# Where the operands of the split products lie in SBUF: staggered slots of 520 columns, weight buffers of 1032

## The chip, the cores and the metric

The kernel runs on one core of one Trainium2 chip. The metric is the device time of one execution in microseconds (us).

## The reference

Two layers of a decoder trunk over 512 tokens of 1024 features, and a last RMSNorm, all in float32. In each layer:

```
n = RMSNorm(h)
p = n @ W_in                                  # 1024 -> 4256 columns
y_A = RWKV7_time_mix(p_A) @ W_oA              # 8 heads x 64, delta-rule state
y_B = MLA(p_B) @ W_oB                         # 8 heads, low-rank q / kv, causal softmax
h = h + (sigmoid(g_A) * y_A + sigmoid(g_B) * y_B) @ W_out
u_gate, u_val = split(RMSNorm(h) @ W_ffn_up)  # 1024 -> 2 x 2816
h = h + (gelu(causal_conv3(u_gate) + b) * u_val) @ W_ffn_down   # 2816 -> 1024
```

## The kernel before, in words

Features lie on the 128 partitions and tokens along the free dimension, so a matrix of activations is a row of tiles of 128x512. Every large product (W_in, the up- and output projections, W_out, the two products of the FFN) is a **split product**: both operands are cut into a high part that TensorE's float32r form holds exactly and a low part, the rest, and one product of a 128x128 weight block with a 128x512 tile of activations becomes three matmuls, `hi·whi`, `lo·whi`, `hi·wlo`, which `mm3` issues in this order (lines 246, 247, 248). In each of them the weight block is the operand loaded into the array (LDWEIGHTS, engine PEld in the profile), and the activations are the 512 columns that stream through it.

**Weights** come from DRAM in units of eight blocks (128x1024 float32), in the order of use. `produce` loads a unit into `raw` (line 209, queue SP), ScalarE rounds it into `whi` (line 201), VectorE subtracts to get `wlo` (line 202). `raw`, `whi` and `wlo` have two buffers each in the pool `wts`. `unit` keeps one unit ahead of the one in use. The last three units of the program (`HELD`) go into slots of the activations' pool, as the last output tile is taken in two halves of 256 tokens.

**Activations** are split by `split` (lines 261 to 269): ScalarE writes `hi`, VectorE writes `lo`. The slots come from the pool `xop` under the tags `xa` and `xb` (8 slots each: the normalised input of the layer and of the FFN, query and kv latents, the outputs of the recurrence and of the attention, and, for the last units, weights), from `mg` under `mop` (16 slots, the operands of W_out) and from `ff` under `hid` (44 slots, the operands of the second FFN product). `wah` in the pool `ta` holds the operands of two small products.

**Stages.** In each layer the mixer's tasks are interleaved by hand. Then come the two output projections, W_out, the first FFN product (22 gate and 22 value tiles of 8 blocks each, with convolution, GELU and product on VectorE, ScalarE and GpSimd beside it) and the second FFN product: 8 output tiles, each of 22 blocks times three matmuls, whose activations are the `hid` slots. In the profile the first FFN product takes about 484 to 700 us (layer 0) and 1300 to 1515 us (layer 1), the second one about 700 to 825 and 1515 to 1640 us.

In the pool `ff` the `hid` slots stand behind seven slots `ft` of 520 columns (2080 bytes a partition) each.

Of the kernel before, what the change touches and what calls it, by code (L numbers as in the profile page):

```python
# [9 lines left out]
F32 = mybir.dt.float32  # L10
F32R = mybir.dt.float32r
# [4 lines left out]
DRAM = bass.MemoryType.DRAM  # L16
# [57 lines left out]
def _blocks(w):  # L74
    """[K, M] -> [K/128 * M/128 blocks of 128 x 128], output tile by output tile."""
    k, m = w.shape
    return w.reshape(k // 128, 128, m // 128, 128).transpose(2, 0, 1, 3).reshape(-1, 128, 128)
# [12 lines left out]

# the last operands of w_out come late: its first tiles leave them to the end
_W_OUT_ORDER = ([(m, k) for m in range(3) for k in range(6)] + [(m, k) for m in range(3) for k in range(6, 8)]
# [3 lines left out]
def _stream(a, l):  # L96
    """All weights of one layer as blocks of 128 x 128 in the order of their use, 8 to a unit."""
    out = []
    w = a["w_in"][l]

    def tiles(idx):
        if not idx:
            return np.zeros((0, 128, 128), np.float32)
        return _blocks(np.concatenate([w[:, i] for i in idx], axis=1))

    out.append(tiles(_W_IN_RWKV[:2]).reshape(2, 8, 128, 128).transpose(1, 0, 2, 3).reshape(16, 128, 128))
    out.append(tiles([_W_IN_GATE[i] for i in GATES[5]]))
    lora = np.concatenate([np.concatenate([a["w_decay_up"][l], a["w_iclr_up"][l]], 0), a["w_gate_up"][l]], 1)
    out.append(lora.reshape(128, 8, 128).transpose(1, 0, 2))
    for p in range(4):  # L110
        if p == 0:
            out.append(tiles(_W_IN_RWKV[2:5]))
        out.append(tiles(_W_IN_RWKV[5 + 3 * p:8 + 3 * p] + [_W_IN_GATE[i] for i in GATES[p]]))
    out.append(tiles(_W_IN_MLA))
    out.append(tiles([_W_IN_GATE[i] for i in GATES[4]]))
    kv = a["w_kv_up"][l].reshape(128, 8, 128)
    kv = np.concatenate([kv[:, :, :64].reshape(128, 512), kv[:, :, 64:].reshape(128, 512)], 1)
    out.append(kv.reshape(128, 8, 128).transpose(1, 0, 2))
    q = a["w_q_up"][l].reshape(256, 8, 96)
    q = np.concatenate([q, q[:, :, 80:96], q[:, :, 64:80]], 2).reshape(256, 1024)  # L120
    out.append(_blocks(q))
    om, ow = _blocks(a["w_out_mla"][l]), _blocks(a["w_out_rwkv"][l])
    out += [ow, om]
    wo = _blocks(a["w_out"][l])
    out.append(wo[[8 * m + k for m, k in _W_OUT_ORDER]])
    up = a["w_ffn_up"][l]
    g, v = _blocks(up[:, :FFN]), _blocks(up[:, FFN:])
    for i in range(FT):
        out += [g[8 * i:8 * i + 8], v[8 * i:8 * i + 8]]
    out.append(_blocks(a["w_ffn_down"][l]))  # L130
    return np.concatenate(out, 0)
# [3 lines left out]
NUNITS = DEPTH * NUNIT  # L135
# units of the last tile of the last product, which is taken in two halves of its tokens
HELD = 3
# [21 lines left out]
def build(ctx, tc, x, pos, wst, vecd, constd, out):  # L159
    nc = tc.nc  # L160
    V, A, G, PE = nc.vector, nc.scalar, nc.gpsimd, nc.tensor
# [33 lines left out]

    # ---- weight stream: units of 8 blocks, split into high and low parts ahead of their use
    state = {"next": 0}
    ready = []

    def parts(r, hi, lo):  # L200
        A.copy(hi, r)  # L201
        V.tensor_tensor(lo, r, hi.bitcast(F32), ALU.subtract)  # L202
        return hi, lo

    def produce():
        u = state["next"]
        state["next"] = u + 1
        raw = wp.tile([128, 1024], F32, name="raw", tag="raw", bufs=2)
        nc.sync.dma_start(raw, wst[u])
        if u >= NUNITS - HELD:  # L210
            # the operands' slots are free by then: these units stay
            tag = "xa" if u < NUNITS - 1 else "xb"
            ready.append([parts(raw[:, c:c + 512], *[xp.tile([128, 512], F32R, name=n, tag=tag, bufs=8)
                                                     for n in ("whi", "wlo")]) for c in (0, 512)])
        else:
            hi, lo = [wp.tile([128, 1024], F32R, name=n, tag=n, bufs=2) for n in ("whi", "wlo")]
            ready.append([parts(raw, hi, lo)])
# [6 lines left out]
    class Blocks:  # L224
        """Hands out 128 x 128 weight blocks in stream order."""

# [29 lines left out]
    def acc():  # L256
        return accp[-1].tile([128, 512], F32, name="acc", tag="acc")

    def split(pool, src, scale, tag, bufs=None):
        """src * scale -> exact high and low operands."""  # L260
        hi = pool.tile([128, 512], F32R, name="hi", tag=tag, bufs=bufs)
        lo = pool.tile([128, 512], F32R, name="lo", tag=tag, bufs=bufs)
        if scale is None:
            A.copy(hi, src)
            V.tensor_tensor(lo, src, hi.bitcast(F32), ALU.subtract)
        else:
            A.activation(hi, src, AF.Copy, scale=scale)  # L267
            V.scalar_tensor_tensor(lo, src, scale, hi.bitcast(F32), ALU.mult, ALU.subtract)
        return hi, lo
# [7 lines left out]
    def rsqrt_bc(ps, n, eps, mul=None, out=None, pst=stat, js=range(4)):  # L277
        """ps[:, js] (sums by token, blocks of 128) -> (ps / n + eps) ** -0.5 on all partitions"""
        v = sm.tile([128, 8], F32, name="nv", tag="nv", bufs=2)
        a, b = js[0], js[-1] + 1  # L280
        c = slice(128 * a, 128 * b)
        V.tensor_scalar(v[:, a:b], ps[:, a:b], 1.0 / n, eps, ALU.mult, ALU.add)  # L282
        G.tensor_tensor(v[:, 4 + a:4 + b], v[:, a:b], mhalf[:, a:b], ALU.pow)  # L283
        w = sm.tile([128, 512], F32, name="nw", tag="nsq", bufs=1)
        A.copy(w[:, c].rearrange("p (j n) -> p j n", n=128), v[:, 4 + a:4 + b, None].to_broadcast([128, b - a, 128]))
        pb = pst()
        for j in js:
            PE.transpose(pb[:, 128 * j:128 * j + 128], w[:, 128 * j:128 * j + 128], ident)
        if out is None:
            return pb  # L290
        if mul is None:
            A.copy(out, pb)
        else:
            V.tensor_tensor(out, pb, mul, ALU.mult)
        return out
# [5 lines left out]
    class Norm:  # L301
        """Sums of squares over the features; add() takes them tile by tile."""

# [19 lines left out]

    # ---- rotary tables
    def rope(T):
# [21 lines left out]

    # ---- scratch in DRAM
    gate_d = dp.tile([16, 128, 512], F32, name="gate_d")
# [4 lines left out]

    # derived vectors
    der = []
# [11 lines left out]
    def load_x(hp):  # L368
        """Loads x, splits it and sums its squares."""
        hs = []  # L370
        ops = []
        for m in range(KT):
            if m % 4 == 0:
                raw, hi, lo = [wp.tile([128, 1024], F32R if n != "raw" else F32, name=n, tag=n, bufs=2)
                               for n in ("raw", "whi", "wlo")]
                ready.append([])
# [15 lines left out]
    def mixer(l, ops, nrm, wks):  # L392
        with ExitStack() as mx:
# [8 lines left out]
            with pool(name=f"ta{l}", bufs=2) as ta, pool(name=f"pa{l}", bufs=2, space=PSUM) as pa, \  # L402
# [66 lines left out]
                def pair(p):  # L469
                    """Two heads, in steps between which other work is put."""  # L470
                    k = shifted(2 + 3 * p, "k")
# [4 lines left out]
                    for i, (w, xx) in enumerate(((0, 0), (0, 1), (1, 0))):  # L476
                        sl = slice(128 * p, 128 * p + 128)
                        PE.matmul(pw, lw[w][0:64, sl], wah[xx][0:64, :], start=i == 0, stop=i == 2)
                        PE.matmul(pq, lw[w][64:128, sl], wah[xx][64:128, :], start=i == 0, stop=i == 2)
                    # log decay sums inside each chunk, P = their exponentials  # L480
                    z = TL("z")
# [19 lines left out]
                    V.tensor_tensor(m, m, k, ALU.mult)  # L501
                    # normalised key direction, negated
                    sq = T("sq")
# [43 lines left out]
                    yield  # L547
                    # chunk matrices
                    for hf in range(2):
# [45 lines left out]
            with pool(name=f"ti{l}", bufs=2) as ti:  # L595
                # ---- latents of the attention
                tabs = []
# [28 lines left out]

                # ---- A_ak V, into the rows of U
                for i in range(4):
# [9 lines left out]

                # ---- (I - A)^-1: blocks of 32 by substitution, then joined to 64
                X = ti.tile([128, 32, 32], F32, name="X", bufs=1)  # L640
# [35 lines left out]

                # ---- chunk recurrence
                St = [None]
# [39 lines left out]
            with pool(name=f"tb{l}", bufs=2) as tb:  # L718
# [5 lines left out]

                # ---- outputs of the chunks
                def chunk_out(i):
# [20 lines left out]

                # group norm, tokens on partitions
                def group_norm(i):
# [42 lines left out]

                # ---- latent attention
                wkv = W.whole()
# [58 lines left out]
                for f in (outputs, norms, lambda: heads(0), lambda: heads(1), transposed, lambda: heads(2), lambda: heads(3)):  # L853
                    f()
                # ---- gated outputs of the recurrence, in the place of AM
                gas = []
# [112 lines left out]
```

## Time and profile before

| | |
|---|---|
| time, median of 2 runs | 1652.89 us (1650.61 and 1655.17) |
| span of the profiled execution | 1654.1 us |
| PE busy / PEld busy | 1593.0 us (96%) / 1271.2 us (77%) |
| DVE, ACT, POOL busy | 959.5, 645.2, 275.4 us |
| the three lines of `mm3` in the chain that ended last | 72% of the span |

The two timed runs of the table are all the times there are of the whole execution; the profiled one is known by its span, from its first to its last instruction. Busy times are those of instructions; a matmul's record is longer than the distance to the next one, since matmuls are pipelined, so the pace of PE is read from how many stand in a stretch of time, not from the length of one. A line is that of the kernel; all three-part products have the lines 246 to 248, so stages are told apart by stretches of time.

### The profile page before, as it was taken

Reading aid. Unit: us, or ns where it says so; the run is one execution under the profiler, and the core shown is the slowest. Engines: PE = TensorE matmul, PEld = TensorE weight load, DVE = VectorE, ACT = ScalarE, POOL = GpSimd, SP = SyncE. Lnnn points to the kernel's source line nnn. Section 1 sums busy time; section 2 is a strip of 40 time slices with the busy share of each in tenths; the row PEclk is TensorE's granted clock in tenths of the full one; section 3 lists DMA queues with packets and bytes.
Section 4 is the critical chain, followed back from the end, with each engine's and each line's share of the span. In section 5 each row is a group of like instructions: output and inputs, shape, how many; then the busy total and the mean of one; then the engine's idle time right before and its main releaser. Section 6 shows DMA issues by size and latency. Waiting matters only on the chain.

```text
span 1654.1 us, 22422 instructions
## 1 busy us (share of the span) xinstructions
PE 1593.0 (96%) x9014; PEld 1271.2 (77%) x9014; DVE 959.5 (58%) x1448; ACT 645.2 (39%) x987; POOL 275.4 (17%) x246
## 2 busy tenths in 40 slices
PE   8999989999999999999999998899999999999997
PEld 6877766668888888888877777766688888888886
DVE  6668885666546555533348669747565555554333
ACT  6334333573433333322234333336634433333222
POOL 2333212400211011100023332123003111110000
PEclk9999989999999999999999999899999999999998
DMA  5323312314423233233342222223244233323232
GB/s 201 111 88 104 102 65 71 116 46 136 145 90 102 90 101 97 95 110 113 108 146 96 83 83 96 71 73 95 69 141 128 88 98 95 102 89 102 90 102 78
DMA packets 57849, 166.09 MB, mean 100 GB/s; under 512 B 6416, under 2 KB 9616, under 8 KB 57744
## 3 DMA queue, kind: packets, MB, share of 16 engines
q1 hardware_dynamic: 57600, 164.48, 31.0%
q8 instruction: 71, 1.16, 0.3%
q14 instruction: 34, 0.28, 0.1%
q10 hardware_dynamic: 144, 0.16, 0.0%
HBM read 147.32 MB, written 17.30 MB: 100 GB/s over the span
## 4 chain that ended last, share of the span: by engine, by line
PE 85%; DVE 10%; issue 2%; ACT 1%; POOL 1%; DMA 1%; SPq 0%; POOLq 0%; DVEq 0%; ACTq 0%
PE acc L246 24%; PE acc L247 24%; PE acc L248 24%; DVE wlo L202 3%; PE sc L830 2%; PE po L848 2%; PE pt L841 1%; PE xy L696 1%; DVE X L644 1%; DVE tm L648 1%; DVE AM L653 1%; POOL nv L283 1%; DVE X L650 1%; PE m L553 1%; DVE z L485 1%
## 5 line engine op out<-in xcount | busy, mean ns | idle before, releaser
L246 PE MATMUL acc<-hi,whi 128*128 128x512 f32 (+1 forms) x1910 | 755.7, 396 | 5.3 <-ACT hi L267 5.3
L248 PE MATMUL acc<-hi,wlo 128*128 128x512 f32 (+1 forms) x1910 | 748.9, 392 | 1.9 <-DVE wlo L202 1.8
L247 PE MATMUL acc<-lo,whi 128*128 128x512 f32 (+1 forms) x1910 | 750.6, 393 | 0.0
L201 ACT CAST whi<-raw 128x1024 fp32r<-128x1024 f32 (+2 forms) x249 | 253.3, 1019 | 569.1 <-PE acc L247 530.5
L202 DVE TENSOR_TENSOR wlo<-raw,whi 128x1024 fp32r<-128x1024 f32 (+2 forms) x249 | 327.5, 1319 | 188.9 <-ACT whi L201 188.1
L246 PEld LDWEIGHTS acc<-hi,whi 128*128 128x128 f32 x1910 | 362.4, 190 | 82.1 <-ACT hi L267 5.3
L248 PEld LDWEIGHTS acc<-hi,wlo 128*128 128x128 f32 x1910 | 361.7, 189 | 80.6 <-DVE wlo L202 3.6
L247 PEld LDWEIGHTS acc<-lo,whi 128*128 128x128 f32 x1910 | 362.2, 190 | 74.3 <-issue 0.7
L920 POOL TENSOR_TENSOR c<-c,rstd 128x512 f32<-128x512 f32 x44 | 57.3, 1304 | 378.0 <-ACT c L919 378.0
L913 DVE TENSOR_TENSOR u<-acc,rstd 128x512 f32<-128x512 f32 x44 | 30.3, 691 | 99.9 <-PE acc L248 94.1
L922 DVE TENSOR_TENSOR c<-c,acc 128x512 f32<-128x512 f32 x44 | 30.2, 687 | 82.4 <-POOL c L920 82.4
L437 POOL TENSOR_TENSOR gg<-gg,rstd 128x512 f32<-128x512 f32 x32 | 52.0, 1625 | 121.2 <-ACT gg L433 121.2
L919 ACT ACTIVATE c<-c 128x512 f32<-128x512 f32 x44 | 27.6, 632 | 78.7 <-DVE c L918 78.7
L315 POOL TENSOR_TENSOR nacc<-nacc,nsq 128x512 f32<-128x512 f32 x14 | 25.1, 1790 | 197.6 <-ACT nsq L314 197.6
L283 POOL TENSOR_TENSOR nv<-nv,cst 128x4 f32<-128x4 f32 (+1 forms) x10 | 14.4, 1440 | 234.5 <-DVE nv L282 234.5
L418 DVE TENSOR_TENSOR cur<-acc,rstd 128x512 f32<-128x512 f32 x28 | 19.2, 691 | 47.9 <-PE acc L248 42.1
L830 PE MATMUL sc<-K,q 128*128 128x128 f32 (+3 forms) x128 | 45.3, 449 | 0.0
L836 ACT ACTIVATE P<-P,mn 128x128 f32<-128x128 f32 (+3 forms) x64 | 35.5, 556 | 16.7 <-DVE mn L833 12.9
L553 PE MATMUL m<-AR,BK 64*128 64x128 f32 x256 | 25.4, 324 | 17.3 <-DVE AM L556 17.3
L833 DVE CUSTOM_DVE_ANT_0 P<-sc,cst 128x128 f32<-128x128 f32 (+3 forms) x64 | 30.4, 482 | 16.6 <-PE pt L841 9.7
L438 ACT ACTIVATE gg<-gg 128x512 f32<-128x512 f32 x32 | 20.2, 632 | 45.4 <-POOL gg L437 45.4
L848 PEld LDWEIGHTS po<-PT,Vt 128*64 128x64 f32 x320 | 22.0, 136 | 20.7 <-issue 8.8
(232 smaller groups left out, 1499.9 us busy)
## 6 DMA issues: line engine op xcount, KB each, us to landing
raw<-in_w SPq DMA_DIRECT2D x238, 512.0 KB, 3.4
gate_d<-gg SPq DMA_DIRECT2D x32, 256.0 KB, 2.4
AM<-gate_d SPq DMA_DIRECT2D x16, 256.0 KB, 4.1
gb<-gate_d SPq DMA_DIRECT2D x16, 256.0 KB, 3.7
h<-in_x SPq DMA_DIRECT2D x8, 256.0 KB, 4.5
rgate_d<-gt SPq DMA_DIRECT2D x8, 256.0 KB, 2.6
bl_d<-rk SPq DMA_DIRECT2D x8, 256.0 KB, 2.0
bl<-bl_d SPq DMA_DIRECT2D x8, 256.0 KB, 2.7
```

The costliest lines, as they stand in the source:

```text
L201: A.copy(hi, r)
L202: V.tensor_tensor(lo, r, hi.bitcast(F32), ALU.subtract)
L246: PE.matmul(ps, w[0], xx[0], start=first, stop=False)
L247: PE.matmul(ps, w[0], xx[1], start=False, stop=False)
L248: PE.matmul(ps, w[1], xx[0], start=False, stop=last)
L283: G.tensor_tensor(v[:, 4 + a:4 + b], v[:, a:b], mhalf[:, a:b], ALU.pow)
L437: G.tensor_tensor(gg, gg, rstd, ALU.mult)
L553: PE.matmul(pA[hh][:, c * 128:c * 128 + 128], BK[64 * hh:64 * hh + 64, 4 * hf + c, :], AR[p][64 * hh:64 * hh + 64, 4 * hf + c, :], start=T ...
L830: PE.matmul(sp[:, 0:n], qs[hh][:, 128 * b:128 * b + 128], ks[hh][:, 0:n], start=True, stop=True)
L836: A.activation(P[:, 0:n], P[:, 0:n], AF.Exp, bias=mn[:, 0:1], scale=-1.0, accum_out=mn[:, 1:2])
L848: PE.matmul(po[64 * hh:64 * hh + 64, 128 * b:128 * b + 128], Vt[:, kb, 64 * hd:64 * hd + 64], PTs[hh][:, 128 * kb:128 * kb + 128], start=k ...
L920: G.tensor_tensor(cc, cc, rstd, ALU.mult)
```

## The change

Three things change in the layout of SBUF, and nothing else.

- `split`, and the last three weight units, take their slots through a new helper, `staggered`. A slot has 520 columns in place of 512 (2080 bytes in place of 2048), and the 512 columns that are used begin 0, 2, 4 or 6 columns into it. The place goes up with every second call, so the `hi` and `lo` of one operand begin equally far in, and the next operand two columns further.
- `whi` and `wlo` have 1032 columns in place of 1024, of which the first 1024 are used.
- Docstrings and comments are gone, and lines behind 258 stand seven further down.

```
+    steps = [0]
+
+    def staggered(pool, name, tag, bufs):
+        o = 2 * (steps[0] // 2 % 4)
+        steps[0] += 1
+        return pool.tile([128, 520], F32R, name=name, tag=tag, bufs=bufs)[:, o:o + 512]
+
     def split(pool, src, scale, tag, bufs=None):
-        hi = pool.tile([128, 512], F32R, name="hi", tag=tag, bufs=bufs)
-        lo = pool.tile([128, 512], F32R, name="lo", tag=tag, bufs=bufs)
+        hi, lo = staggered(pool, "hi", tag, bufs), staggered(pool, "lo", tag, bufs)
...
     # produce
-            ready.append([parts(raw[:, c:c + 512], *[xp.tile([128, 512], F32R, name=n, tag=tag, bufs=8)
+            ready.append([parts(raw[:, c:c + 512], *[staggered(xp, n, tag, 8)
                                                      for n in ("whi", "wlo")]) for c in (0, 512)])
         else:
-            hi, lo = [wp.tile([128, 1024], F32R, name=n, tag=n, bufs=2) for n in ("whi", "wlo")]
+            hi, lo = [wp.tile([128, 1032], F32R, name=n, tag=n, bufs=2)[:, 0:1024] for n in ("whi", "wlo")]
...
     # load_x
-                raw, hi, lo = [wp.tile([128, 1024], F32R if n != "raw" else F32, name=n, tag=n, bufs=2)
+                raw, hi, lo = [wp.tile([128, 1024 if n == "raw" else 1032], F32R if n != "raw" else F32, name=n, tag=n, bufs=2)
```

The built programs hold the same instructions in the same order on every engine, with the same waits and the same buffer for each tile. What differs is where in a partition the tiles begin. Counted in bytes from a multiple of 64, the built programs have:

| operand | before | after |
|---|---|---|
| weight block `whi`, `wlo` (both buffers) | 32 | 32 in one buffer, 0 in the other |
| activations `hi`, `lo` in `xa`, `xb`, `mop` | 32 | 0, 8, ... 56, all eight places |
| activations `hi`, `lo` in `hid` | 0 | 0, 8, ... 56, all eight places |

In the program before, every `whi`, `wlo`, `hi` and `lo` of the three-part products begins at a multiple of 32 bytes, and the distance from weight block to activations, modulo 64, is 0 in 4632 of the 5778 matmuls and 32 in 1146 (the second FFN product, and the gate's small product with `wah`). In the changed program this distance takes each of the eight values 0, 8, ... 56 in 712 to 732 matmuls, and the `hi` and the `lo` of one operand lie 32 bytes apart by this count everywhere (47456 and 62016, or 59944 and 57864, for the first two operands), since neighbouring slots of 2080 bytes do.

## The prediction

> **What bounds the kernel now.** I read the page's busy times first, then its chain, then the pace of the matmuls stage by stage. In the page, busy us and share of the span stand behind each engine; the chain gives shares of the span.
>
> ```profile
> span 1654.1 us, 22422 instructions
> PE 1593.0 (96%) x9014; PEld 1271.2 (77%) x9014; DVE 959.5 (58%) x1448; ACT 645.2 (39%) x987; POOL 275.4 (17%) x246
> ...
> PE 85%; DVE 10%; issue 2%; ACT 1%; POOL 1%; DMA 1%; SPq 0%; POOLq 0%; DVEq 0%; ACTq 0%
> PE acc L246 24%; PE acc L247 24%; PE acc L248 24%; DVE wlo L202 3%; PE sc L830 2%; PE po L848 2%; PE pt L841 1%; PE xy L696 1%; DVE X L644 1%; DVE tm L648 1%; DVE AM L653 1%; POOL nv L283 1%; DVE X L650 1%; PE m L553 1%; DVE z L485 1%
> ```
>
> TensorE is the bound, and 72% of the span (0.72 x 1654.1 = 1191 us) are the three lines of `mm3`, whose operands the change moves. So what counts is the distance from one such matmul to the next. A record is longer than that distance, so I take it from counts: (stretch + one record) / matmuls in it. Columns: stretch, its length, PE busy and count, granted clock, DMA.
>
> ```profile
> core 0: us, PE busy (x), PEclk, DMA share, GB/s
> 385.00:475.00 90.00, 90.00 (x398) 1.00 0.43 135
> 490.00:690.00 200.00, 200.00 (x885) 1.00 0.31 98
> 1200.00:1280.00 80.00, 80.00 (x354) 1.00 0.45 134
> 1310.00:1500.00 190.00, 190.00 (x839) 1.00 0.31 98
> 710.00:820.00 110.00, 110.00 (x473) 1.00 0.35 112
> 1530.00:1620.00 90.00, 90.00 (x387) 1.00 0.31 97
> ```
>
> The second row gives 200.389 / 885 = 0.2264, the fifth 110.395 / 473 = 0.2334, the last 90.395 / 387 = 0.2336 us. PE is 100% busy in all six and the clock is 1.00, yet the pace is one of two: 0.2267 in the first four, 0.2333 in the last two, which are the second FFN product. The records say the same; first three rows a stretch of the first FFN product, last three of the second:
>
> ```profile
> L246 PE MATMUL acc<-hi,whi 128*128 128x512 f32 x148 | 57.6, 389 | 0.0
> L247 PE MATMUL acc<-lo,whi 128*128 128x512 f32 x148 | 57.6, 389 | 0.0
> L248 PE MATMUL acc<-hi,wlo 128*128 128x512 f32 x147 | 57.2, 389 | 0.0
> ...
> L246 PE MATMUL acc<-hi,whi 128*128 128x512 f32 x144 | 56.9, 395 | 0.0
> L248 PE MATMUL acc<-hi,wlo 128*128 128x512 f32 x143 | 56.5, 395 | 0.0
> L247 PE MATMUL acc<-lo,whi 128*128 128x512 f32 x143 | 56.5, 395 | 0.0
> ```
>
> 389 against 395 ns: 6 to 7 ns a matmul, with nothing waiting (last column 0.0). Form, shape, order and weight buffers are the same in both. What differs is the place: in the second FFN product the activations begin 0 bytes into 64 and the weights 32, elsewhere both 32. So the trace of before already holds a trial of this change's idea, and the **unlike** pair is the slower one. It isn't proof: the `hid` slots also lie higher in SBUF.
>
> A second view speaks for the same. After PE has been held up, the first matmuls of a run are slow too, though their places are alike:
>
> ```profile
> 380.71 0.39 PE L248 MATMUL acc<-hi,wlo 128*128 128x512 f32 x1
> ...
> 381.87 0.39 PE L247 MATMUL acc<-lo,whi 128*128 128x512 f32 x1
> ...
> 383.00 0.39 PE L246 MATMUL acc<-hi,whi 128*128 128x512 f32 x1
> ```
>
> Between the first two rows lie five distances, 1.16 / 5 = 0.232 us; between the last two again five, 1.13 / 5 = 0.226. So a run of matmuls with like places falls into step after some five of them, and until then goes at about the pace of the second FFN product. I read this as two streams, activations and the next weight block, that get into each other's way unless they hold a fixed relation. That reading is an inference; the two paces are measured.
>
> **The change part by part.** How many matmuls it touches:
>
> ```profile
> L246 PE MATMUL acc<-hi,whi 128*128 128x512 f32 x1866 | 743.4, 398 | 5.3 <-ACT hi L267 5.3
> ...
> L246 PE MATMUL acc<-hi,whi 128*128 128x256 f32 x44 | 12.4, 281 | 0.0
> ```
>
> 3 x 1866 = 5598 of 512 columns and 3 x 44 = 132 halves (48 more, under other tile names, I leave out). The second FFN product has 8 tiles x 22 x 3 = 528 in layer 0 and 7 x 22 x 3 = 462 in layer 1, together 990 at 0.2333; the other 4608 go at 0.2267 once in step. All of it: 4608 x 0.2267 + 990 x 0.2333 + 132 x 0.117 (half of 0.2333) = 1044.6 + 231.0 + 15.4 = 1291 us, of which the chain holds 1191: 92% of a change in pace reaches the end.
>
> *Staggered activations and the weight buffers' 32 bytes* have one answer together. After the change the `hi` and `lo` of an operand lie 32 bytes apart everywhere, and `mm3` issues `hi`, `lo`, `hi`: whatever relation holds for one matmul, the next has another one by half of 64 bytes. A run of five like ones, which the rows above need to fall into step, never comes. So I expect all 4608 to go at 0.2333, as the second FFN product does, and that one to stay as it is.
> - Upper end: 4608 x 6.67 ns x 0.92 = 28 us.
> - Lower end: only those that are in step for certain lose, those of the first four stretches: 398 + 885 + 354 + 839 = 2476 x 6.67 ns = 16.5 us. The rest is interrupted often (the row above has a mean of 398 ns over the program, not 389), so part of it is out of step now.
> - I take the middle, **+22 us**.
>
> What could lie outside these ends is in the rivals, since no row shows an activation that begins 8, 16 or 24 bytes into a multiple of 32.
>
> *The engines that write the operands.* VectorE and ScalarE now write `hi` and `lo` at places that are no multiple of 32 bytes. The nearest rows are those of the convolution, which reads the same tile from its first column (L918) and from its second (L917), and writes two columns in (L913) or from the first (L922):
>
> ```profile
> L918 DVE SCALAR_TENSOR_TENSOR c<-u,vec,c 128x512 f32<-128x512 f32 x20 | 15.0, 751 | 0.6
> ...
> L917 DVE SCALAR_TENSOR_TENSOR c<-u,vec,c 128x512 f32<-128x512 f32 x19 | 14.2, 746 | 0.0
> L922 DVE TENSOR_TENSOR c<-c,acc 128x512 f32<-128x512 f32 x20 | 13.7, 687 | 37.1 <-POOL c L920 37.1
> L913 DVE TENSOR_TENSOR u<-acc,rstd 128x512 f32<-128x512 f32 x18 | 12.5, 692 | 44.2 <-PE acc L248 44.2
> ```
>
> 751 against 746 and 687 against 692 ns: 5 ns either way. The six stretches above had PE at 100%, so this lies beside it. Nothing.
>
> *Order, waits, transfers.* No instruction, wait, buffer or DMA moves; the units' loads stay 512 KB each. Nothing, and the cover is ample: a unit feeds 24 matmuls, 24 x 0.2267 = 5.4 us, and lands in
>
> ```profile
> raw<-in_w SPq DMA_DIRECT2D x238, 512.0 KB, 3.4
> ```
>
> 3.4 us; at twenty-four times 0.2133 it would still have 5.1.
>
> **The skill on this.** The Trainium skill, "SBUF — State Buffer", section "Who interferes with whom", says that TensorE has one read port for the moving operand and an independent one for weight loads, and that PE never waits on anyone in SBUF. By that rule the places can't matter and the time stays at 1653 us. The rows of 389 and 395 ns, with one form and one clock, speak against it, as far as place is what differs there.
>
> **The rivals.**
>
> *Like places are the trouble (faster).* A pace of 0.2267 may have room below it. The program's first matmuls stand evenly and nearly twice as far apart as later ones:
>
> ```profile
> 7.15 0.63 PE L246 MATMUL acc<-hi,whi 128*128 128x512 f32 x1
> ...
> 9.71 0.63 PE L246 MATMUL acc<-hi,whi 128*128 128x512 f32 x1
> ```
>
> Six distances: 2.56 / 6 = 0.4267 us, half of which is 0.2133. If those are the half-clock pace of a stream without stalls (an estimate: the clock's records begin later), 13.3 ns of each 226.7 are stalls, and 20.0 of each 233.3. If steps of two columns keep the two streams out of each other's way, all of it goes: (4608 x 13.3 + 990 x 20.0) ns x 0.92 = 75 us, to 1578; half of it gives 1615. It takes effect as soon as the mean distance falls under 0.225. For it: every pair in before lies at a multiple of 32 bytes, so 8, 16 and 24 are untried. Against it: the one distance that was tried, 32, is worse than 0, and in the slow start shown above, where the two streams are still shifting against each other, the pace comes down to 0.226 and stops there.
>
> The Trainium skill, "TensorE: Matmul & The Clock Gate", section "Wait — 56ns, not 53.3ns?", gives 215.7 ns between back-to-back matmuls of 512 columns at full clock. By its figure the room is 11.0 and 17.6 ns, an estimate of 63 us in all.
>
> *Little happens (no change).* Either the pace of the second FFN product has another cause, such as where its slots lie in SBUF, or a matmul's pace hangs on its own pair alone, not on those before it. In the second case the pairs, spread over all eight distances, go at 0.230 on average: 4608 x 3.3 ns x 0.92 = +14, less 990 x 3.3 ns x 0.92 = -3. Together 0 to +11 us, 1653 to 1664. For it: 0 and 32 are the only distances known, and a mean is what a spread gives. Against it: the five slow matmuls after each break show that the past counts.
>
> *A broken first line costs by itself (slower).* An activation that begins inside a line touches one line more. If the stream is bound by lines, three of four operands (those begun 2, 4 or 6 columns in) pay one more: by lines of 64 bytes 226.7 / 32 = 7.1 ns, on 0.75 x 5598 matmuls, x 0.92 = 27 us on top of the 22, to 1702. It decides as soon as a broken line costs more than 3 ns, where the total passes 2%. For it: the stream has no slack, as its pace answers to places at all. Against it: activations that begin 32 into 64 break a line too if lines have 64 bytes, and they are the fast ones.
>
> **How the numbers follow.** Out of step everywhere: 0.45. Little happens: 0.20. Faster: 0.21. Broken lines: 0.14. The span of 1654.1 us lies 1.2 above the median of the runs shown (1652.89), so the likeliest is 1654.1 + 22 - 1 = **1675 us**; its own ends are 1669 and 1681. For 8 in 10 the range takes in the milder halves of both outer cases: **1600 to 1705**. 2%, about what a measurement of this kernel can tell from no change, is 33 us, so the likeliest case, a loss of 1.3%, counts as within it with most of its weight: 0.38 of its 0.45 (the rest is slower), with 0.20 for little happening and 0.02 from the mildest of the faster case, 0.60. Slower: 0.07 + 0.14 = 0.21. Faster: 0.19.
>
> **What would show it.** In the profile after: the count of matmuls in a stretch of the first FFN product (885 in 200 us before; 859 if out of step, 939 without stalls), the mean record there (389 before; 395 expected) and in the second FFN product (395, expected the same). If both products show 389, the pair of like halves was the whole matter; if the second falls to 389 and the first rises, each pair counts alone. Records over 400 would mean broken lines. PE's busy share, the order and the waits should stay. I am wrong if the two streams don't meet in SBUF at all, or if 8 bytes are enough to part them.

## The result and the profile after

The changed kernel takes 1677.87 us (median of 2 runs, 1677.24 to 1678.49) against 1652.89 before: 1.0149 of before, 95% interval 1.0114 to 1.0184. The prediction was 1675. From its page and its groups of instructions, the rows that answer to those shown of before:

```profile
span 1675.4 us, 22422 instructions
PE 1614.7 (96%) x9014; PEld 1277.0 (76%) x9014; DVE 960.0 (57%) x1448; ACT 642.8 (38%) x987; POOL 275.0 (16%) x246
...
L246 PE MATMUL acc<-hi,whi 128*128 128x512 f32 x1866 | 750.5, 402 | 5.2 <-ACT hi L274 5.2
```

Span and PE's busy time grew by the same 21 to 22 us; VectorE, ScalarE and GpSimd did not move. The pace, in the six stretches of the prediction (columns as there):

```profile
385.00:475.00 90.00, 90.00 (x389) 1.00 0.42 131
490.00:690.00 200.00, 198.97 (x859) 1.00 0.30 95
1200.00:1280.00 80.00, 80.00 (x368) 1.00 0.44 137
1310.00:1500.00 190.00, 188.81 (x822) 1.00 0.29 94
710.00:820.00 110.00, 110.00 (x476) 1.00 0.34 110
1530.00:1620.00 90.00, 90.00 (x390) 1.00 0.29 94
```

The first FFN product has 859 matmuls in 200 us where it had 885, at the same clock. (The stages come 5 to 22 us later than before, so the third stretch takes in other matmuls, and the second and the fourth have a break of about 1 us inside them; read the pace from the rest.) The second product went the other way: 476 in 110 us after 473, and 390 in 90 after 387. The two paces of before have become one, close to the slower. The mean records are 395, 394 and 394 ns for the three lines in the first product (389 before), and 393 to 394 in the second (395 before). From the start of every 512-column matmul of `mm3` to the next in the timeline, breaks left out, the mean is 228.4 ns before (5286 of them) and 231.95 after (5256). 3.5 ns x 5778 matmuls (132 of them halves) = 20 us of the 21.

By stage, from the first such matmul of one to that of the next in the two timelines (the first mixer from the start of the span, the last product to its last matmul):

| stage | before, us | after, us | difference |
|---|---|---|---|
| mixer with output projections, layers 0 and 1 | 415.0 and 408.6 | 420.2 and 412.2 | +8.9 |
| W_out, both | 43.5 and 43.5 | 44.6 and 44.5 | +2.1 |
| first FFN product, both | 242.2 and 242.2 | 248.1 and 247.6 | +11.3 |
| second FFN product, both | 123.2 and 124.8 | 122.4 and 124.5 | -1.1 |

In the profile of before the first FFN product begins at 458.5 us in layer 0 and 1276.0 us in layer 1; the 484 and 1300 us given further up are its first break. The mixer's 8.9 us are not clear of noise: e11 and e12 below leave the mixer of layer 0 with one and the same layout, and it took 406.5 us in one and 416.3 in the other. Its pace, breaks left out, is surer: 228.1 ns a matmul before and 231.9 after, over some 1800 matmuls each, which makes about 7 us.

### The profile page after: what moved, and what is told of

Read it like the earlier page. It is cut to its first block, busy times and chain, and to the rows that moved or that the text cites. A ratio compares the mean times of both kernels' runs of the same rounds, so it can differ in the third digit from the quotient of the medians.

```text
span 1675.4 us, 22422 instructions
## 1 busy us (share of the span) xinstructions
PE 1614.7 (96%) x9014; PEld 1277.0 (76%) x9014; DVE 960.0 (57%) x1448; ACT 642.8 (38%) x987; POOL 275.0 (16%) x246
## 4 chain that ended last, share of the span: by engine, by line
PE 86%; DVE 10%; issue 2%; ACT 1%; POOL 1%; DMA 1%; SPq 0%; POOLq 0%; DVEq 0%; ACTq 0%
PE acc L246 25%; PE acc L247 25%; PE acc L248 24%; DVE wlo L202 3%; PE sc L837 2%; PE po L855 2%; PE pt L848 1%; PE xy L703 1%; DVE X L651 1%; DVE tm L655 1%; DVE AM L660 1%; PE m L560 1%; POOL nv L290 1%; DVE X L657 1%; DVE z L492 1%
## 5 line engine op out<-in xcount | busy, mean ns | idle before, releaser
L247 PE MATMUL acc<-lo,whi 128*128 128x512 f32 (+1 forms) x1910 | 759.2, 397 | 0.0
```

What stands on the lines that cost most here:

```text
L247: PE.matmul(ps, w[0], xx[1], start=False, stop=False)
```

## The experiments

All of them are changes of the kernel before. "Distance" is the place of the activations less that of the weight block, in bytes.

**Is it distance, place or height?** `e1_hid_like` moves the `hid` slots to the weights' place modulo 64; `e2_shift_all` moves weights and activations by 32 bytes, all but the slots `mop` of W_out, whose pool is laid out from the other end of SBUF and stays where it was.

```
+                fp.tile([128, 8], F32, name="pad", bufs=1)      # e1, first in the pool "ff"
+    cp.tile([128, 8], F32, name="pad")                          # e2, first in the pool "const"
```

> Before, with eight unused columns ahead of the pool of the second FFN product, so that its activations begin 32 bytes into 64 like the weights (distance 0 in nearly all three-part products). Theory A (the pace hangs on the distance between weight block and activations modulo 64, and a run of equal distances 0 falls into step at 0.2267 us): the second FFN product goes from 0.2333 to 0.2267 us a matmul, 430 to 442 in 100 us, and the time falls by 990 x 6.7 ns plus 132 halves x 3.3 ns = 7 us, to about 1646. Theory B (the slots are slower because they lie high in SBUF): 0.2333 stays, 1653.

> Before, with eight unused columns ahead of everything: all operands move by 32 bytes. Weights at 0, most activations at 0, those of the second FFN product at 32, so every distance is as before. Theory A (distance counts): paces as before, 0.2267 in the first FFN product and 0.2333 in the second, 1653 us. Rival (the absolute place of the activations counts, 32 good, 0 bad): the paces change places, 0.2333 in the first and 0.2267 in the second, about 1675.

Second FFN product of before and of e1:

```profile
725.00:815.00 90.00, 90.00 (x388) 1.00 0.35 111
725.00:815.00 90.00, 90.00 (x395) 1.00 0.36 117
```

First and second FFN product of e2, then a stretch of W_out in before and in e2:

```profile
490.00:690.00 200.00, 200.00 (x884) 1.00 0.30 96
725.00:815.00 90.00, 90.00 (x388) 1.00 0.35 111
418.00:456.00 38.00, 38.00 (x170) 1.00 0.44 137
418.00:456.00 38.00, 38.00 (x164) 1.00 0.44 138
```

e1: 90.39 / 395 = 0.2288 us, where before has 388 in the same stretch, 0.2330. Faster, so height isn't what made the second product slow; but not the 0.2267 of theory A. The time went to 0.9975 of before (0.9957 to 0.9993), 1649.45 us. e2: both paces of the FFN stay, with both operands moved by 32: the place by itself, at multiples of 32, isn't it. W_out shows the other half. Its activations did not move and the weights did, so its distance went from 256 to 224, against the expectation that every distance stays, and its pace from 226.7 ns to 233.3 (start to start). So it is the distance, but modulo 64 is too coarse: in e1 it is 0 modulo 64 and 64 modulo 256.

**Does a constant distance do?** Slots of 528 columns, begun `o` columns in: 2 and 4 (e3), 6 and 8 (e4) in layers 0 and 1.

```
-        hi = pool.tile([128, 512], F32R, name="hi", tag=tag, bufs=bufs)
-        lo = pool.tile([128, 512], F32R, name="lo", tag=tag, bufs=bufs)
+        o = begin[0]
+        hi, lo = [pool.tile([128, 528], F32R, name=n, tag=tag, bufs=bufs)[:, o:o + 512] for n in ("hi", "lo")]
...
```

> Slots of 528 columns (2112 bytes, so hi and lo lie alike), begun 2 columns in for layer 0 and 4 for layer 1; weights as before. Distances are constant over a stage: 8 in layer 0's first FFN product and 40 in its second, 16 and 48 in layer 1's. Theory A as I put it (only distance 0 falls into step): about 0.232 in all four. Rival (any constant distance falls into step): 0.2267 in all four but perhaps not in 40. Rival (a distance that is no multiple of 32 parts the two streams): below 0.2267, down to 0.2133, in one or more of the four, and 1600 to 1640 us.

> The same with 6 columns in layer 0 and 8 in layer 1: distances 24 (first FFN product) and 56 (second) in layer 0, 32 and 0 in layer 1. Theory A: 0.232 for 24, 56 and 32, and 0.2267 for layer 1's second FFN product, the reverse of before in that layer. Rival (any constant distance falls into step): 0.2267 for 24 and 56. Rival (no multiple of 32 parts the streams): below 0.2267 for 24 or 56.

First and second FFN product of layer 0, then of layer 1; e3, then e4:

```profile
490.00:690.00 200.00, 198.80 (x847) 1.00 0.29 92
725.00:815.00 90.00, 90.00 (x385) 1.00 0.34 111
1325.00:1500.00 175.00, 175.00 (x756) 1.00 0.29 94
1545.00:1625.00 80.00, 80.00 (x347) 1.00 0.29 93
```

```profile
490.00:690.00 200.00, 198.81 (x856) 1.00 0.29 92
725.00:815.00 90.00, 90.00 (x388) 1.00 0.34 113
1325.00:1500.00 175.00, 175.00 (x751) 1.00 0.29 94
1545.00:1625.00 80.00, 80.00 (x348) 1.00 0.31 99
```

No stage falls into step: (198.80 + 0.39) / 847 = 0.2352 is the slowest, the others lie at 0.231 to 0.235. Neither rival holds, and 0 modulo 64 (last row of e4) isn't enough either, for which theory A had expected 0.2267. These distances are constant modulo 64 only: slots of 2112 bytes shift it by 64 modulo 256 from one to the next. The times, 1680.53 and 1678.62 us (one run each), are those of the changed kernel. It needs no staggering at all to lose what it lost.

**Which part of the change costs?** e5 has the slots of 520 columns alone, all begun at column 0; e6 has the weight buffers of 1032 alone. These push what lies behind them: in the built program of e6 the activations of the first FFN product lie 128 bytes further, and the distances there are 128, 96, 64 and 32 modulo 256. None is 0, unlike what the expectation of e6 says.

> The change's slots of 520 columns, all begun at their first column, with before's weight buffers: hi and lo lie 32 bytes apart, no 8, 16 or 24. Theory A with memory (one unlike neighbour spoils the step): about 0.232 us everywhere, 1672 to 1678 as after the change. Rival (each matmul goes by its own pair, 0 fast, 32 slow): two fast to one slow or the reverse, 0.229 to 0.231, 1660 to 1668. Rival (only the begin inside 32 bytes costs): 0.2267 as before, 1653.

> The change's weight buffers of 1032 columns alone, activations as before: the distance modulo 64 is constant for the 24 matmuls of a unit and alternates from unit to unit. Theory A modulo 64: units in turn at 0.2267 (after some five) and 0.2333, 0.230 in the mean, about 1665. As the first runs showed 0.2289 and 0.2311 at distances that are 0 modulo 64 but not modulo 128, theory A2 is that the distance must be 0 modulo 256: the other weight buffers lie 32, 64 and 96 bytes further, so only hi times whi of every other unit keeps 0, and the pace is about 0.232, 1672 to 1678.

First FFN product of layer 0, e5 and e6:

```profile
490.00:690.00 200.00, 200.00 (x862) 1.00 0.28 92
```

```profile
490.00:690.00 200.00, 198.82 (x861) 1.00 0.29 92
```

0.2325 and, leaving out the break of 1.2 us, 0.2314 us (0.2320 from start to start). Times: 1.0139 of before (1.0107 to 1.0170) and 1.0151 (1.0115 to 1.0187). **Each alone costs what the whole change costs, 1.0149; they do not add.** Either one takes most pairs away from the distance 0, so there is little left for the other to spoil. The begin of 2, 4 or 6 columns adds nothing measurable to the slots' own loss. In e5, the matmuls whose own distance is 0 modulo 256 stand 230.5 ns from the next in the mean (603 of them), not 226.7: neighbours count as well. e6 goes against the theory modulo 64 (0.230), with A2.

**The map of distances.** The `hid` operands of one layer lie in one tile, 2048 bytes apart, so the distance is constant modulo 512 for 24, 24 and 18 matmuls in a row, in each of the eight output tiles. Where a group begins nearer to its slot's start than the one before, its first high part overwrites up to 120 columns of the low part before it (one operand in layer 1 of e7, one in each layer of e8).

```
+                hb = fp.tile([128, 44 * 512 + 128], F32R, name="hid", bufs=1)
-                    hops.append(split(fp, cc, None, "hid", 44))
+                    o = [[32, 124, 113], [110, 8, 112]][l][i // 8]      # e8
+                    hi, lo = [hb[:, 512 * j + o:512 * j + o + 512] for j in (2 * i, 2 * i + 1)]
...
```

> Before, with the second FFN product's activations in one tile, 2048 bytes apart, so that the distance to the weight block is constant modulo 512 for a group of operands (8, 8 and 6 operands of each output tile, 24, 24 and 18 matmuls in a row). Layer 0: 8, 16, 24. Layer 1: 32, 64, 128. Theory A2 (only distances that are 0 modulo 256 fall into step at 0.2267): 0.229 to 0.236 in all six groups. Rival (128 is enough): 0.2267 at 128. Rival (constancy is enough): 0.2267 wherever the distance is constant. Rival (like places are the trouble): some distance with less than 0.2267. Time about 1653 in any case, 5 us either way.

> The same with distances 192, 48 and 4 in layer 0 and 504, 96 and 0 in layer 1. Theory A2: 0.2267 in the last group of layer 1 alone, 0.229 to 0.236 in the others. Rival (near enough to 0 is enough): 0.2267 at 4 and 504 as well. Rival (like places are the trouble): less than 0.2267 somewhere.

The first matmuls of groups in the timeline (start, record), e7: those of 8, 16, 24 and the next, then of 64, 128, 32 and the next.

```profile
744.17 0.40 PE L246 MATMUL acc<-hid,whi 128*128 128x512 f32 x1
749.75 0.39 PE L246 MATMUL acc<-hid,whi 128*128 128x512 f32 x1
755.31 0.39 PE L246 MATMUL acc<-hid,whi 128*128 128x512 f32 x1
759.52 0.40 PE L246 MATMUL acc<-hid,whi 128*128 128x512 f32 x1
...
1566.78 0.39 PE L246 MATMUL acc<-hid,whi 128*128 128x512 f32 x1
1572.28 0.39 PE L246 MATMUL acc<-hid,whi 128*128 128x512 f32 x1
1576.45 0.39 PE L246 MATMUL acc<-hid,whi 128*128 128x512 f32 x1
1582.04 0.39 PE L246 MATMUL acc<-hid,whi 128*128 128x512 f32 x1
```

e8: those of 4, 192, 48 and the next; then of 504, 96 and 0; then, inside the group of 0, its tenth, and the first of the next group.

```profile
756.57 0.39 PE L246 MATMUL acc<-hid,whi 128*128 128x512 f32 x1
760.85 0.39 PE L246 MATMUL acc<-hid,whi 128*128 128x512 f32 x1
766.44 0.39 PE L246 MATMUL acc<-hid,whi 128*128 128x512 f32 x1
771.97 0.39 PE L246 MATMUL acc<-hid,whi 128*128 128x512 f32 x1
...
1563.44 0.40 PE L246 MATMUL acc<-hid,whi 128*128 128x512 f32 x1
1569.01 0.40 PE L246 MATMUL acc<-hid,whi 128*128 128x512 f32 x1
1574.62 0.39 PE L246 MATMUL acc<-hid,whi 128*128 128x512 f32 x1
...
1576.70 0.39 PE L246 MATMUL acc<-hid,whi 128*128 128x512 f32 x1
...
1578.74 0.40 PE L246 MATMUL acc<-hid,whi 128*128 128x512 f32 x1
```

Start to start over the matmuls between, in ns (the means over all output tiles lie within 0.4 of these):

| distance modulo 512 | 0, settled | 4 | 8 | 16 | 24 | 32 | 48 | 64 | 96 | 128 | 192 | 504 |
|---|---|---|---|---|---|---|---|---|---|---|---|---|
| ns a matmul | 226.7 | 237.8 | 232.5 | 231.7 | 233.9 | 232.9 | 230.4 | 229.2 | 233.8 | 231.7 | 232.9 | 232.1 |

The group of 0 takes 2.08 / 9 = 231 ns at first and 2.04 / 9 = 226.7 in its second half: it falls into step within the group. No other one does, not even 4 or 504. W_out, whose distance is 256 modulo 512, has 226.7 in these two runs and before, in the mean of its starts. The other pairs 256 apart agree as well: 288 (before) has 233.3 and 32 has 232.9, 320 (e1) has 228.9 and 64 has 229.2. So the fast place is **0 modulo 256**, and no distance that was tried goes below 226.7 at full clock. At the distances 4, 8, 16, 24, 48 and 504 the activations also begin off a multiple of 32 bytes, which e11 and e12 take up.

**The version for the fast place.** e9 puts 56 unused columns ahead of the pool "ff", where e1 had 8; `hid` then has distance 0 modulo 512.

> Before, with 56 unused columns ahead of the pool of the second FFN product, so that its activations lie at the weights' place modulo 512 bytes, not only modulo 64 as in the first trial (0.2289 there). Theory A2 (distance 0 modulo 256 falls into step): the second FFN product at 0.2267 us like the first, 990 x 6.7 ns + 132 x 3.3 ns = 7 us less, 1646 to 1648, below before and below the first trial. Rival (the second product has a floor of its own at 0.2289): as the first trial, 0.9975 of before.

First FFN product and second:

```profile
490.00:690.00 200.00, 200.00 (x884) 1.00 0.29 97
725.00:815.00 90.00, 90.00 (x399) 1.00 0.34 111
```

90.39 / 399 = 0.2265: the second product is as fast as the first. Time 1646.89 us, 0.9951 of before (0.9932 to 0.9970), 8 us for one line that computes nothing. It beats both kernels.

**Is it the weights' bytes?** e10 lets two of three weight loads read half as much.

```
-        PE.matmul(ps, w[0], xx[1], start=False, stop=False)
+        PE.matmul(ps[0:64], w[0][:, 0:64], xx[1], start=False, stop=False)
...
```

`hi·wlo` is halved in the same way, except in the last block of a tile.

> Before, with lo times whi, and hi times wlo except in the last block of a tile, taken for output rows 0 to 63 alone: two of three weight loads read 64 columns in place of 128 (the low parts of rows 64 to 127 are left out). Activations stream 512 columns as before. Theory (the stalls come from weight loads and activations meeting in SBUF): fewer stalls, 0.218 to 0.223 us in the first FFN product, and the gap between the two FFN products shrinks. Rival (the stream of activations alone makes them, by its own place): 0.2267 and 0.2333 as before. Time 1600 to 1630 by the theory, 1653 by the rival.

First FFN product, second, and a weight load of each size:

```profile
490.00:690.00 200.00, 200.00 (x873) 1.00 0.29 95
725.00:815.00 90.00, 90.00 (x388) 1.00 0.33 109
...
L246 PEld LDWEIGHTS acc<-hi,whi 128*128 128x128 f32 x146 | 27.4, 188 | 13.2
L247 PEld LDWEIGHTS acc<-lo,whi 128*64 128x64 f32 x145 | 19.4, 134 | 6.0
```

The loads got shorter (188 to 134 ns), the pace did not: 0.2295 in the first product, out of step, and 0.2330 in the second, as before. The theory expected 0.218 to 0.223 and falls; its rival, 0.2267 and 0.2333, holds for the second product alone. The time of the one run was 1666.18 us, where the theory had at most 1630. Fewer weight bytes alone did not make it faster. As the sizes of loads alternate here and did not before, the run doesn't tell what the bytes do when the form stays.

**Does the begin inside 32 bytes count?** e11: in layer 0 the change's steps of 0, 2, 4, 6 columns alone; in layer 1 weights and activations both 2 columns in. e12: in layer 0 both 4 columns in; in layer 1 only the weights, 2.

```
+            b = 2 if u >= NUNITS - FT else 0                                       # e11
+            hi, lo = [wp.tile([128, 1088], F32R, name=n, tag=n, bufs=2)[:, b:b + 1024] for n in ("whi", "wlo")]
+                    o = 48 + (2 * (i % 4) + 64 * (i // 4) if l == 0 else 2)        # e11
...
```

The weight buffers of 1088 columns put the distances of the first FFN product at 0 and 256 modulo 512 in turn, half of the matmuls each.

> Before, with the second FFN product changed: in layer 0 its activations begin 0, 2, 4, 6 columns in, operand by operand (distances 0, 8, 16, 24 modulo 256, the change's step alone); in layer 1 the activations and the weights both begin 2 columns in (distance 0, but no multiple of 32 bytes), up to the three last units. Theory A2 (distance counts, and a change of distance spoils the step): layer 0 at 0.2315 to 0.2335, layer 1 at 0.2267. Rival (a begin inside a line costs by itself): layer 1 at 0.230 to 0.234.

> As the run before, with the second FFN product's places changed again: in layer 0 weights and activations both begin 4 columns (16 bytes) in, distance 0 modulo 256; in layer 1 the activations begin at a multiple of 32 bytes and the weights 2 columns behind one (up to the three last units), distance 248. The run before showed 0.2333 with both 2 columns in, against the theory that the distance alone counts. Theory A3 (distance 0 modulo 256 and a begin at a multiple of 32 bytes are both needed): 0.229 to 0.234 in both layers. Rival (a multiple of 16 bytes is enough): 0.2267 in layer 0. Rival (only the activations' begin has to be a multiple of 32, the weights' may be off it): 0.2267 in layer 1.

First FFN product of e11, then the second of layers 0 and 1 of e11, then of e12:

```profile
490.00:690.00 200.00, 200.00 (x884) 1.00 0.30 97
725.00:815.00 90.00, 90.00 (x388) 1.00 0.34 112
1520.00:1600.00 80.00, 80.00 (x345) 1.00 0.28 92
```

```profile
725.00:815.00 90.00, 90.00 (x393) 1.00 0.33 109
1520.00:1600.00 80.00, 80.00 (x348) 1.00 0.29 96
```

The first product keeps its pace (884 as in e2 and e9), so a change between 0 and 256 does not spoil the step. The steps alone: 90.39 / 388 = 0.2330, as out of step as the rest of the change. Both 2 in: 80.40 / 345 = 0.2330, though the distance is 0; here theory A2 fails. Both 4 in: 90.39 / 393 = 0.2300; weights alone 2 in: 80.39 / 348 = 0.2310. So of the places tried only those have the fast pace that have both: distance 0 modulo 256, and begins at a multiple of 32 bytes. Both of e12's rivals fall. Which operand's begin counts isn't told: at distance 0 both are off a multiple of 32 together, and with the weights alone off, the distance is 248.

**Does it hold at half clock?** Both kernels have short stretches in the mixers with a granted clock of 0.50. A stretch and two of its matmuls, before and after:

```profile
246.15:249.10 2.95, 2.95 (x8) 0.50 0.00 0
...
246.14 0.63 PE L248 MATMUL acc<-hi,wlo 128*128 128x512 f32 x1
248.70 0.60 PE L248 MATMUL acc<-hi,wlo 128*128 128x512 f32 x1
...
1077.61:1080.60 2.99, 2.99 (x9) 0.50 0.00 0
...
1077.60 0.63 PE L247 MATMUL acc<-lo,whi 128*128 128x512 f32 x1
1080.16 0.63 PE L247 MATMUL acc<-lo,whi 128*128 128x512 f32 x1
```

In both, six distances from start to start take 2.56 us, 426.7 ns each. Before, the operands lie 0 modulo 256 apart there; after, the seven matmuls of the stretch lie 120, 24, 0, 32, 192, 200 and 232 apart. But for the first after a break, all neighbours in such stretches, 40 before and 51 after, stand 426 to 427 ns apart. So at half clock the places do not matter, and what they cost, they cost at full clock.

## Why the prediction was right, point by point

- *TensorE bounds, and the pace of `mm3` decides.* Shown: 3.5 ns more a matmul, 21 us more in the span, no other engine moved.
- *The unlike pair of the second FFN product is a trial of the change.* Right, and shown by e1 and e9: 0.2330, 0.2288, 0.2265 as its distance goes from 288 to 320 to 0 modulo 512. Wrong in the grain: modulo 64 is not the rule.
- *All 4608 go to 0.2333, the second product stays; +22 us.* The sum is right in part by luck, as two errors cancel. The loss is 5.3 ns a matmul (226.7 to 232), not 6.67; but it falls on all stages but the second product, the mixer too, which the middle of the two ends had partly written off: the three stages lost 8.9 + 2.1 + 11.3 us, and the second product gained 1.1. The count of 859 is the forecast one by luck too: the stretch has a break of 1 us, and by the mean of 232.4 ns there (start to start) 200.39 us without it hold 862.
- *The cause I gave, the alternation of `hi` and `lo` by 32 bytes.* Half right. Neighbours count (e5's 230.5 ns at distance 0), but the alternation isn't needed: in e7 and e8 the distance is constant and nothing but 0 falls into step. "Some five" matmuls to fall into step was read from one run of them; it took nine in e8, and four to ten after breaks in the mixers of before.
- *"Two streams that get into each other's way".* Not shown. e10 speaks against the simplest form of it. What is measured is the dependence on the distance, at full clock alone; why it has a period of 256 bytes and what is stalled stays open. In the sweeps the next weight block, which is loaded meanwhile, lies like the own one modulo 512, so they don't tell which of the two counts.
- *Writers at odd places cost nothing.* VectorE's busy time went from 959.5 to 960.0, ScalarE's from 645.2 to 642.8.
- *The rivals.* "Like places are the trouble": no distance went below 226.7 at full clock. The estimate that 0.4267 us is a half-clock pace is borne out by the stretches at clock 0.50; that 213.3 ns can be had at full clock isn't. "Little happens" by pairs that count alone: distances spread, as that rival said, but their mean is 232, not 230, since 0 modulo 256 is one of 32, not 0 modulo 64 one of eight. "A broken first line": e11 shows that a begin inside 32 bytes spoils the step, but no stage of the changed kernel shows the 7 ns on top; the 237.8 ns at distance 4 is the only one that comes near. Lines of 64 bytes, from which the 7 ns came, are shown by no run.

## What to carry to other kernels

In a kernel bound by float32r matmuls of 512 columns, give weights and activations slots whose distances are multiples of 256 bytes and that begin at multiples of 32, and look for stages whose count of matmuls per microsecond is 3% below another's at the same clock and with nothing waiting: an odd-sized tile ahead of a pool is enough to shift it. The pad of e9 cost nothing and is worth trying before any restructuring. Spreading the begins of the operands, as the change does, made the kernel slower.

## What the runs showed of the hardware that was not expected

- The pace of float32r matmuls hangs on the distance of the two operands in SBUF: 226.7 ns at 0 modulo 256 with begins at multiples of 32, 229 to 238 at the other places tried. At a granted clock of 0.50 it doesn't: 426.7 ns at each place that occurred there.
- It takes a run of like pairs to get there: nine matmuls at 231 ns, then nine at 226.7 (e8).
- Halving two of three weight loads made the first FFN product slower, 226.7 to 229.5 ns (e10).
- The Trainium skill ("SBUF — State Buffer", section "Who interferes with whom") has TensorE waiting on no one in SBUF. With one program order and a clock of 1.00 in both, e9 and before differ by 6 to 7 ns a matmul in the second FFN product; for the places of TensorE's own two operands the measurement decides, and no run here shows it waiting on another engine.
